# A decoder block on one core: two homes for the transposed softmax weights, a slot order with later transposes, and memory operands formed early in the space of input and residual

## The chip, the core and the metric

The kernel runs on one core of a Trainium2 chip. A core has five engines, each with its own queue, which it works off in order: TensorE (PE in the profile, its weight loads PEld), VectorE (DVE), ScalarE (ACT), GpSimd (POOL) and SyncE (SP), which here issues most of the transfers between HBM and the on-chip memory SBUF. TensorE writes its results to PSUM banks, from which VectorE and ScalarE evacuate them. The metric is the device time of one execution in microseconds; less is better.

## What is computed

One layer of a decoder block on a sequence of 512 tokens of width 1024, cut to what matters:

```python
u = rmsnorm(h, g_mix)
qa, ka, va, qb, kb, vb = split(u @ w_in, 6)
ya = dilated_attention(qa, ka, va)       # 8 heads of 64
yb = moba_attention(qb, kb, vb)          # 8 heads of 64, block 256
y = concat(rmsnorm(ya, g_out_dil), rmsnorm(yb, g_out_moba))
h = h + y @ w_out
# cross attention, 4 heads of 256, over 256 memory tokens
km, vm = split(rmsnorm(mem, g_mem) @ w_kv_mem, 2)
h = h + softmax(rmsnorm(h, g_cross) @ w_q @ km.T / 16) @ vm @ w_o
h = h + (silu(conv3(f @ w_gate)) * (f @ w_up)) @ w_down   # f = rmsnorm(h, g_ffn)
out = rmsnorm(h, g_final)
```

Everything is float32. Each product is made of three matmuls in the faster number format fp32r: an operand is split into a high part (a rounded copy, made by ScalarE) and a low part (the operand less its high part, made by VectorE or GpSimd), and high x high, high x low and low x high are summed in PSUM.

## The kernel before

The data lie transposed: features on the 128 partitions, the 512 tokens along the free axis. The input x is loaded into the eight tiles of `h`, which stay for the whole kernel as the residual; `X` holds their scaled high and low parts. Weights come in chunks of 128 x 1024 through the class `Weights`: SP loads a chunk into one of three `stage` buffers (line 74), ScalarE makes `hi` (line 88), VectorE or GpSimd makes `lo` (line 97); a chunk is loaded when the one three places earlier has been split.

Work that follows a matmul group is not written behind it but put into `Later` (lines 140 to 170): a chain of stages, each with a due step. TensorE's program calls `step()` after each small piece of work, and stages that are due are emitted then, into the queues of their engines. `need(token)` emits until a stage is out.

The attention is a software pipeline of 18 slots (line 780). In slot s three generators take turns: `s_steps(s)` makes the scores of head s in three pieces and puts the softmax into `Later` (a0 reduces on VectorE, a1 is the exponential on ScalarE, a2 the reciprocal and scaling; the last piece is scaled by GpSimd, line 695); `t_steps(s-1)` transposes the softmax weights of head s-1 in three groups (line 710, TensorE), with a copy by ScalarE (the high part) and a subtraction by VectorE (the low part, line 254) behind each; `o_steps(s-2)` multiplies the transposed weights of head s-2 with V in four pieces (line 739). The string `ORDER` says whose turn it is at each of the ten places of a slot. Ahead of each place `fill` runs some pieces of other work (an eighth of a unit, mostly three matmuls), as the table `PACE` demands: the projections `qk_unit` and `vb_unit` of later heads, and at the end, from about slot 11 on, the memory units `km_unit` (line 561) and `vm_unit` (lines 588 to 590). Accumulators of these units take turns in two PSUM banks (`acc`); scores, transposes and outputs share six others.

The memory operands are the memory, transposed and scaled, split into high and low parts. They are formed in `mem_prep` from two raw chunks, that pass through the `stage` buffers, into the tiles `X`, when the last projection (the unit k7) has read its eighth of X: one copy by ScalarE and one operation by VectorE (line 261, `X<-stage`) for each of the eight.

After the slots come the output projection with both group norms (its first addition to `h` is GpSimd's, line 832, the second VectorE's, line 840), cross attention, the feed-forward part and the final norm. These are not changed.

Of the kernel before, what the change touches and what calls it, by code (L numbers as in the profile page):

```python
# [11 lines left out]
F32 = mybir.dt.float32  # L12
# [4 lines left out]
P = 128  # L17
# [14 lines left out]
ORDER = "OSOTOSTOST"  # L32
# [140 lines left out]
def block_kernel(tc, xT, x_tok, memT, mem_tok, w_in, w_out, w_q, w_km, w_vm, w_o, w_gu, w_dn, vecs, relT, onehot,  # L173
                 addend, out):
    nc = tc.nc
    with ExitStack() as ctx:
        perm = ctx.enter_context(tc.tile_pool(name="perm", bufs=1))
        wp = ctx.enter_context(tc.tile_pool(name="wp", bufs=1))
# [24 lines left out]
        chunks += [(memT[0], "raw"), (memT[1], "raw")]  # L203
# [14 lines left out]
        hh_ = perm.tile([P, KT, S], F32, name="h")  # L218
        h = [hh_[:, k, :] for k in range(KT)]
        nc.scalar.dma_start(vec, vecs)  # L220
        nc.sync.dma_start(h[0], xT[0])
        W.dma(0)
        nc.sync.dma_start(h[1], xT[1])
        W.dma(1)
        for k in (2, 3):
            nc.sync.dma_start(h[k], xT[k])
# [17 lines left out]
        def col(c):  # L244
            return vec[:, c:c + 1]
# [121 lines left out]
        def x_split(k):  # L367
            copy(Xh[k], h[k], col(C_MIX + k))
            scaled_lo(Xl[k], h[k], col(C_MIX + k), Xh[k])
# [40 lines left out]
        for k in range(KT):  # L410
            if k % 2 == 0:
                w = W.take()
            for j in XL.get(k, ()):
                nc.sync.dma_start(h[j], xT[j])
# [29 lines left out]

        Q, K, VM = {}, {}, {}
# [12 lines left out]
        def qk_unit(p, is_k):  # L458
            hook = p == 7 and is_k
            w = W.take()  # L460
            ps = bank("acc")
            for k in range(KT):
                if hook and k == 0:
                    mem_start()
                proj(w, k, ps, Xh[k], Xl[k])
                if hook:
                    L.chain(*mem_prep(k), d=1)
                yield
# [76 lines left out]
        def mem_start():  # L545
            W.lo_eng = tuple(engs[c] for c in LOM)
            VM["st"] = [W.raw(), W.raw()]

        def mem_prep(k):

            src = VM["st"][k // 4][:, (k % 4) * M:(k % 4) * M + M]
            hi, lo = X[k][:, 0, 0:M], X[k][:, 0, M:2 * M]
            return (lambda: copy(hi, src, col(C_MEM + k)),
                    lambda: scaled_lo(lo, src, col(C_MEM + k), hi))

        def km_unit(m):
            w = W.take()
            ps = bank("acc")[:, :M]
            for k in range(KT):
                W.tick(k)  # L560
                fgroup(ps, w, k, X[k][:, 0, 0:M], X[k][:, 0, M:2 * M], k == 0, k == KT - 1)
                if k % 2 == 1:
                    L.step()
                    yield
            hi, lo = X[m][:, 1, 0:M], X[m][:, 1, M:2 * M]
            v = {}

            def e0():
                v["q"] = tmp()[:, :M]
                mul(v["q"], ps, Rm)  # L570

            L.chain(e0, lambda: copy(hi, v["q"]), lambda: sub(lo, v["q"], bf(hi)))

        def vm_unit(c):
# [71 lines left out]
        for u in (qk_unit(0, 0), qk_unit(0, 1)):  # L646
            for _ in u:
# [56 lines left out]
        def t_steps(hh):  # L704
            pt = PT[hh]
            L.need(tok["p", hh])
            for g in range(3):
# [6 lines left out]
                hi, lo = (t[:, o:o + n] for t in pts[g])  # L714
# [14 lines left out]
        def o_steps(hh):  # L729
# [50 lines left out]
        for s in range(18):  # L780
# [6 lines left out]
            if s == 16:  # L787
                ra_tok = L.chain(*norm_stages(SSQ[0], SSQ[0], S, 512), gap=3)
# [8 lines left out]
        att.close()  # L797
        cr = ExitStack()
# [472 lines left out]
```

## Time and profile before

| | |
|---|---|
| time, median of 3 runs | 796.68 us (796.01 to 797.83) |
| the profiled execution | 796.25 us, of which its span (first to last instruction) 794.5 us |
| TensorE (PE) busy | 772.7 us, 97% of the span, 3916 matmuls |
| VectorE (DVE) | 491.7 us, 62% |
| ScalarE (ACT) | 388.7 us, 49% |
| GpSimd (POOL) | 162.6 us, 20% |
| transfers | 85.86 MB, mean 108 GB/s |

Busy time is the time in which an engine has an instruction in work. Matmuls overlap, so a busy TensorE is not one at its peak: what tells whether it waited is the time from the start of one matmul to the start of the next. A row of the timeline gives start, duration, engine, line, operation, what is written and read, and in brackets how long the engine was idle before and which engine and line ended that. The table of waits sums these by waiting and releasing line.

### The profile page before, as it was taken

The page shows a single profiled execution, that of the slowest core. Times are in us where ns is not written, and L with a number is a line of the kernel's source. Part 1 is how long each engine was busy: PE and PEld are TensorE (multiplying, and loading weights), DVE is VectorE, ACT ScalarE, POOL GpSimd, SP SyncE. Part 2 cuts the span into 40 slices and gives each one's busy share as a digit, 9 for nine tenths or more (in the row PEclk, how much of TensorE's full clock was granted, in tenths as well). Part 3 has the DMA queues.
Part 4 walks back from the last instruction along what each step waited for, and adds up shares of the span by engine and source line. Part 5 has one row for each costly group of instructions (what it writes and reads, how often), then busy time and mean ns, then how long its engine had stood idle before and what let it go on. Part 6 is the DMA issues. An engine that isn't in the chain of part 4 may idle for free.

```text
span 794.5 us, 10594 instructions
## 1 busy us (share of the span) xinstructions
PE 772.7 (97%) x3916; PEld 653.9 (82%) x3916; DVE 491.7 (62%) x895; ACT 388.7 (49%) x763; POOL 162.6 (20%) x161
## 2 busy tenths in 40 slices
PE   9999999999999999999999999999999999999995
PEld 7878989877898887888888888888888888888884
DVE  4657676678886987756476765665665664333324
ACT  5856666776767543544355533334333343322322
POOL 1057465663646243000030000000000000000001
PEclk9999999999999999999999999999999999999998
DMA  9545243343534322211232323223223233333303
GB/s 344 198 133 138 78 145 93 109 112 123 161 134 131 108 80 85 75 53 54 80 106 92 104 97 106 99 87 104 91 98 106 88 92 100 99 93 100 99 21 106
DMA packets 27108, 85.86 MB, mean 108 GB/s; under 512 B 3072, under 2 KB 5248, under 8 KB 26672
## 3 DMA queue, kind: packets, MB, share of 16 engines
q1 hardware_dynamic: 25696, 83.90, 32.8%
q10 hardware_dynamic: 1232, 1.12, 0.4%
q8 instruction: 31, 0.51, 0.3%
q14 instruction: 21, 0.17, 0.1%
q0 software_dynamic: 128, 0.17, 0.1%
HBM read 78.84 MB, written 2.14 MB: 102 GB/s over the span
## 4 chain that ended last, share of the span: by engine, by line
PE 77%; DVE 11%; ACT 6%; issue 2%; POOL 2%; DMA 1%; DVEq 0%; POOLq 0%; ACTq 0%
PE acc L267 15%; PE acc L266 15%; PE acc L268 15%; PE s L267 6%; PE s L266 6%; PE s L268 6%; DVE lo L97 2%; ACT P L688 2%; PE o L739 1%; DVE tmp L257 1%; PE t L710 1%; DVE P L695 1%; DVE P L683 1%; ACT hi L88 1%; PE acc L531 1%
## 5 line engine op out<-in xcount | busy, mean ns | idle before, releaser
L88 ACT ACTIVATE hi<-stage 128x512 fp32r<-128x512 f32 (+1 forms) x264 | 151.9, 616 | 173.0 <-PE acc L267 126.6
L97 DVE TENSOR_TENSOR lo<-stage,hi 128x512 fp32r<-128x512 f32 (+1 forms) x211 | 154.8, 764 | 59.4 <-ACT hi L88 59.2
L266 PE MATMUL acc<-X,hi 128*128 128x512 f32 (+1 forms) x416 | 159.5, 384 | 1.1 <-DVE tmp L257 1.1
L268 PE MATMUL acc<-X,lo 128*128 128x512 f32 (+1 forms) x416 | 155.5, 374 | 0.0
L267 PE MATMUL acc<-X,hi 128*128 128x512 f32 (+1 forms) x368 | 137.3, 373 | 1.8 <-DVE X L261 1.5
L268 PEld LDWEIGHTS acc<-X,lo 128*128 128x128 f32 x416 | 78.2, 188 | 14.2
L266 PEld LDWEIGHTS acc<-X,hi 128*128 128x128 f32 x416 | 78.4, 188 | 13.8 <-ACT P L688 1.0
L267 PEld LDWEIGHTS acc<-X,hi 128*128 128x128 f32 x368 | 69.3, 188 | 13.1 <-DVE X L261 3.1
L97 POOL TENSOR_TENSOR lo<-stage,hi 128x512 fp32r<-128x512 f32 x53 | 71.6, 1368 | 27.3 <-ACT hi L88 25.7
L266 PE MATMUL s<-X,hi 128*128 128x512 f32 x192 | 75.1, 391 | 0.0
L268 PE MATMUL s<-X,lo 128*128 128x512 f32 x192 | 74.7, 389 | 0.0
L266 PE MATMUL acc<-G,hi 128*128 128x512 f32 (+1 forms) x198 | 72.9, 368 | 0.0
L268 PE MATMUL acc<-G,lo 128*128 128x512 f32 (+1 forms) x198 | 72.3, 365 | 0.0
L267 PE MATMUL acc<-G,hi 128*128 128x512 f32 (+1 forms) x198 | 72.3, 365 | 0.0
L267 PE MATMUL s<-X,hi 128*128 128x512 f32 x176 | 68.5, 389 | 0.0
L688 ACT ACTIVATE P<-P,st 128x512 f32<-128x512 f32 (+1 forms) x64 | 35.6, 557 | 39.9 <-DVE st L683 39.7
L1072 DVE SCALAR_TENSOR_TENSOR c<-a,vec,c 128x512 f32<-128x512 f32 x44 | 33.1, 752 | 25.2 <-ACT c L1067 24.4
L1062 POOL MEMSET a<- 128x2 f32 x22 | 2.1, 99 | 214.8 <-DVE c L1072 214.0
L266 PEld LDWEIGHTS acc<-G,hi 128*128 128x128 f32 x198 | 37.3, 188 | 6.2
L266 PEld LDWEIGHTS s<-X,hi 128*128 128x128 f32 x192 | 36.0, 187 | 7.7 <-issue 0.2
L268 PEld LDWEIGHTS acc<-G,lo 128*128 128x128 f32 x198 | 37.3, 188 | 6.1
L267 PEld LDWEIGHTS acc<-G,hi 128*128 128x128 f32 x198 | 37.3, 188 | 6.0
(249 smaller groups left out, 1498.8 us busy)
## 6 DMA issues: line engine op xcount, KB each, us to landing
stage<-in_w_gu_dram SPq DMA_DIRECT2D x44, 512.0 KB, 3.3
stage<-in_w_in_dram SPq DMA_DIRECT2D x23, 512.0 KB, 3.5
stage<-in_w_dn_dram SPq DMA_DIRECT2D x16, 512.0 KB, 3.5
strip<-scr SPq DMA_DIRECT2D x16, 256.0 KB, 3.6
stage<-in_w_km_dram SPq DMA_DIRECT2D x8, 512.0 KB, 3.3
stage<-in_w_vm_dram SPq DMA_DIRECT2D x8, 512.0 KB, 3.4
stage<-in_w_out_dram SPq DMA_DIRECT2D x8, 512.0 KB, 3.2
stage<-in_w_q_dram SPq DMA_DIRECT2D x8, 512.0 KB, 3.2
```

The lines of the kernel that those rows point to most:

```text
L88: self.nc.scalar.activation(self.hi[i][:, a:b], self.stage[i][:, a:b], AF.Copy)
L97: self.lo_eng[part].tensor_sub(self.lo[i][:, a:b], self.stage[i][:, a:b], bf(self.hi[i][:, a:b]))
L257: nc.vector.tensor_mul(dst, a, b)
L266: nc.tensor.matmul(ps, wh[:, w0:w0 + P], xh, start=first, stop=False)
L267: nc.tensor.matmul(ps, wh[:, w0:w0 + P], xl, start=False, stop=False)
L268: nc.tensor.matmul(ps, wl[:, w0:w0 + P], xh, start=False, stop=last)
L531: nc.tensor.matmul(ps, Xh[k][:, ts], wh[:, ws], start=(k == 0), stop=False)
L683: nc.vector.tensor_tensor_reduce(v, src, sb[:, :n][:, ::-1], -0.125, 3e38, OP.add, OP.min, accum_out=st[:, i:i + 1])
L688: nc.scalar.activation(v, v, AF.Exp, scale=-1.0, bias=st[:, i:i + 1], accum_out=st[:, 4 + i:5 + i])
L695: engs[NME[i]].tensor_scalar(v, v, st[:, 8 + i:9 + i], None, op0=OP.mult)
L710: nc.tensor.transpose(ps[:, c * P:(c + 1) * P], pt[:, PO[i] + kb * P:PO[i] + (kb + 1) * P], ident)
L1072: nc.vector.scalar_tensor_tensor(v["c"], v["a"][:, 6 + o:6 + o + S], col(C_CW + o * FT + f), v["c"], op0=OP.mult, op1=OP.add)
```

## The change

1. `ORDER` goes from "OSOTOSTOST" to "OOSOOTSTST". With places counted from 0, O stood at 0, 2, 4, 7, S at 1, 5, 8, T at 3, 6, 9; now O stands at 0, 1, 3, 4, S at 2, 6, 8, T at 5, 7, 9.
2. The transposed weights get a second set of tiles; even and odd heads use one each.
3. The memory operands are formed in slots 3 to 7, by the same sixteen operations, but from four loads of 256 KB of their own (tile `mr`, one buffer) and into a tile of their own, `xm`. That tile lies in the space in which the input x lay; after the last memory unit the space is taken by the residual `h`, for which x is loaded a second time (eight transfers of 256 KB on SP's queue). The two raw chunks no longer pass through the `stage` buffers. GpSimd makes both low halves of the weights until the first memory unit begins, not until the unit k7 begins.
4. The norm of the first eight heads has its stages 5 steps apart instead of 3, and the memory set aside for transfers that GpSimd issues is 2048 bytes.

```diff
-ORDER = "OSOTOSTOST"
+ORDER = "OOSOOTSTST"
...
-        chunks += [(memT[0], "raw"), (memT[1], "raw")]
...
-        hh_ = perm.tile([P, KT, S], F32, name="h")
-        h = [hh_[:, k, :] for k in range(KT)]
+        x_ = hp.tile([P, KT, S], F32, tag="H", name="x")
+        x = [x_[:, k, :] for k in range(KT)]
...
+        XM = hp.tile([P, KT, 2 * M], F32R, tag="H", name="xm")
+        def mem_prep(j):
+            v = {}
+            def p0():
+                v["t"] = tp.tile([P, 2 * M], F32, tag="mr", bufs=1, name=f"mr{j}")
+                nc.sync.dma_start(v["t"], memT[j // 2][:, (j % 2) * 2 * M:(j % 2 + 1) * 2 * M])
+            def p1(i):
+                hi, src = XM[:, 2 * j + i, 0:M], v["t"][:, i * M:(i + 1) * M]
+                copy(hi, src, col(C_MEM + 2 * j + i))
+            def p2(i):
+                hi, lo, src = XM[:, 2 * j + i, 0:M], XM[:, 2 * j + i, M:2 * M], v["t"][:, i * M:(i + 1) * M]
+                scaled_lo(lo, src, col(C_MEM + 2 * j + i), hi)
+            L.chain(p0, d=68 + 22 * j)
+            L.chain(lambda: p1(0), lambda: p2(0), lambda: p1(1), lambda: p2(1), d=80 + 22 * j, gap=2)
+        for j in range(4):
+            mem_prep(j)
...
         def qk_unit(p, is_k):
-            hook = p == 7 and is_k
...
-                if hook and k == 0:
-                    mem_start()
                 proj(w, k, ps, Xh[k], Xl[k])
-                if hook:
-                    L.chain(*mem_prep(k), d=1)
...
-                fgroup(ps, w, k, X[k][:, 0, 0:M], X[k][:, 0, M:2 * M], k == 0, k == KT - 1)
+                fgroup(ps, w, k, XM[:, k, 0:M], XM[:, k, M:2 * M], k == 0, k == KT - 1)
...
-        pts = [(ap_.tile([P, 512], F32R, name="pt0h"), ap_.tile([P, 512], F32R, name="pt0l")),
-               (ap_.tile([P, 384], F32R, name="pt1h"), ap_.tile([P, 384], F32R, name="pt1l")),
-               (ap_.tile([P, 512], F32R, name="pt2h"), ap_.tile([P, 512], F32R, name="pt2l"))]
+        pts = [[tuple(ap_.tile([P, n], F32R, name=f"pt{g}{z}{e}") for z in "hl")
+                for g, n in enumerate((512, 384, 512))] for e in range(2)]
...
-                hi, lo = (t[:, o:o + n] for t in pts[g])
+                hi, lo = (t[:, o:o + n] for t in pts[hh % 2][g])
...
-                                     pts[pg][z][:, a:b], start=(kb == 0 and z == 0),
+                                     pts[e][pg][z][:, a:b], start=(kb == 0 and z == 0),
...
-                ra_tok = L.chain(*norm_stages(SSQ[0], SSQ[0], S, 512), gap=3)
+                ra_tok = L.chain(*norm_stages(SSQ[0], SSQ[0], S, 512), gap=5)
...
+        hh_ = hp.tile([P, KT, S], F32, tag="H", name="h")
+        h = [hh_[:, k, :] for k in range(KT)]
+        for k in range(KT):
+            nc.sync.dma_start(h[k], xT[k])
...
-    nc = _bacc.Bacc("TRN2", target_bir_lowering=False, num_devices=1)
+    nc = _bacc.Bacc("TRN2", target_bir_lowering=False, num_devices=1, dynamic_dma_scratch_size=2048)
```

What stands in a row on the engines is shown at three places. Line numbers of the kernel after are 1 to 17 higher. First TensorE in slot 10, where the transposes of head 9 begin (P9 its softmax weights, t a transposes' bank, o the output of head 8, pt its transposed weights, acc a projection). Before:

```order
L739 MATMUL o_127_1742<-pt1h_428,V2_711 128x384
L739 MATMUL o_127_1742<-pt1l_429,V2_711 128x384
L266 MATMUL acc_128_1746<-X2_108,hi21_1559 128x512
L267 MATMUL acc_128_1746<-X2_108,hi21_1559 128x512
L268 MATMUL acc_128_1746<-X2_108,lo21_1590 128x512
L710 MATMUL t_131_1779<-ident_85,P9_1640 128x128 x4
L266 MATMUL acc_128_1746<-X3_109,hi21_1559 128x512
L267 MATMUL acc_128_1746<-X3_109,hi21_1559 128x512
L268 MATMUL acc_128_1746<-X3_109,lo21_1590 128x512
L739 MATMUL o_127_1742<-pt2h_430,V2_711 128x256
L739 MATMUL o_127_1742<-pt2l_431,V2_711 128x256
```

and now:

```order
L752 MATMUL o_127_1778<-pt2h0_434,V2_722 128x256
L752 MATMUL o_127_1778<-pt2l0_435,V2_722 128x256
L267 MATMUL acc_128_1782<-X3_112,hi21_1594 128x512
L268 MATMUL acc_128_1782<-X3_112,hi21_1594 128x512
L269 MATMUL acc_128_1782<-X3_112,lo21_1625 128x512
L752 MATMUL o_127_1778<-pt2h0_434,V2_722 128x256
L752 MATMUL o_127_1778<-pt2l0_435,V2_722 128x256
L267 MATMUL acc_128_1782<-X4_113,hi21_1594 128x512
L268 MATMUL acc_128_1782<-X4_113,hi21_1594 128x512
L269 MATMUL acc_128_1782<-X4_113,lo21_1625 128x512
L723 MATMUL t_132_1834<-ident_88,P9_1687 128x128 x4
```

The first transposes stood behind the second piece of O and the third eighth of the projection (X2); now all four pieces of O and the fifth eighth (X4) stand ahead of them.

Second VectorE, from the evacuation of q7 on (the unit k7 runs on TensorE, and head 12's scores begin). Before, with the memory operations `X<-stage` between the rest:

```order
L254 TENSOR_TENSOR pt2l_431<-t_146_1941,pt2h_430 128x384
L514 TENSOR_TENSOR Q7_1951<-tmp_149_1962,Q7_1951 64x512
L261 SCALAR_TENSOR_TENSOR X0_106<-stage24_1602,vec_71,X0_106 128x256
L261 SCALAR_TENSOR_TENSOR X1_107<-stage24_1602,vec_71,X1_107 128x256
L97 TENSOR_TENSOR lo27_1984<-stage27_1895,hi27_1953 128x512
L261 SCALAR_TENSOR_TENSOR X2_108<-stage24_1602,vec_71,X2_108 128x256
L683 ISA P12_1992,st12_1993<-s_151_1994,strip12_1754 128x512
L683 ISA st12_1993 128x1
L261 SCALAR_TENSOR_TENSOR X3_109<-stage24_1602,vec_71,X3_109 128x256
L693 RECIPROCAL st12_1993<-st12_1993 128x1
L695 TENSOR_SCALAR P12_1992<-P12_1992,st12_1993 128x512
L261 SCALAR_TENSOR_TENSOR X4_110<-stage25_1692,vec_71,X4_110 128x256
```

and now:

```order
L255 TENSOR_TENSOR pt2l0_435<-t_147_1976,pt2h0_434 128x384
L535 TENSOR_TENSOR Q7_1983<-tmp_149_1994,Q7_1983 64x512
L696 ISA P12_2026,st12_2027<-s_151_2028,strip12_1801 128x512
L696 ISA st12_2027 128x1
L706 RECIPROCAL st12_2027<-st12_2027 128x1
L708 TENSOR_SCALAR P12_2026<-P12_2026,st12_2027 128x512
L773 TENSOR_TENSOR y5_2048<-o_150_2008,tmp_152_2049 64x512
L258 TENSOR_TENSOR tmp_154_2063<-acc_148_1984,rx_2_141 128x512
```

The memory operations are gone from here, and the addition y, which ends an output, has come forward to the first scaling.

Third VectorE in slot 15, around the last scores (P15) and the first evacuations of the memory values (vml). Before:

```order
L760 TENSOR_TENSOR y6_2436<-o_191_2485,tmp_199_2592 64x512
L97 TENSOR_TENSOR lo37_2608<-stage37_2425,hi37_2600 128x512
L261 SCALAR_TENSOR_TENSOR Y6_123<-y6_2436,vec_71,Y6_123 128x512
L683 ISA P15_2498,st15_2499<-s_201_2619,strip15_2156 128x128
L683 ISA st15_2499 128x1
L683 ISA P15_2498,st15_2499<-s_201_2619,strip15_2156 128x256
L683 ISA st15_2499 128x1
L693 RECIPROCAL st15_2499<-st15_2499 128x2
L261 SCALAR_TENSOR_TENSOR vml_2512<-acc_197_2567,small_87,vmh_2511 128x256
```

and now:

```order
L773 TENSOR_TENSOR y6_2395<-o_191_2501,tmp_195_2568 64x512
L262 SCALAR_TENSOR_TENSOR Y6_126<-y6_2395,vec_74,Y6_126 128x512
L262 SCALAR_TENSOR_TENSOR vml_2523<-acc_192_2524,small_90,vmh_2522 128x256
L696 ISA P15_2536,st15_2537<-s_199_2596,strip15_2186 128x384
L696 ISA st15_2537 128x1
L255 TENSOR_TENSOR pt0l0_431<-t_196_2577,pt0h0_430 128x512
L706 RECIPROCAL st15_2537<-st15_2537 128x1
L708 TENSOR_SCALAR P15_2536<-P15_2536,st15_2537 128x384
L97 TENSOR_TENSOR lo35_2628<-stage35_2440,hi35_2622 128x512
L255 TENSOR_TENSOR pt1l0_433<-t_200_2609,pt1h0_432 128x384
L696 ISA P15_2536,st15_2537<-s_201_2636,strip15_2186 128x128
```

The addition y6 and the scaling Y6 stood right ahead of the third piece's reductions (128x128 and 128x256); now they stand ahead of the second piece's (128x384).

## Rows read from the trace of the kernel before

**Rows 1.** Busy time by stretch: stretch, PE, PEld, DVE, ACT, POOL, clock, DMA share, GB/s.

```profile
47.00:262.00 215.00, 206.17 (x1312) 183.58 (x1311) 155.54 (x367) 148.52 (x338) 120.39 (x103) 1.00 0.40 123
105.00:165.00 60.00, 59.87 (x356) 52.47 (x355) 41.89 (x101) 39.91 (x94) 35.08 (x32) 1.00 0.39 116
165.00:210.00 45.00, 40.77 (x245) 34.60 (x244) 35.97 (x85) 32.71 (x76) 24.73 (x22) 1.00 0.41 126
```

**Rows 2.** Waits of TensorE: waiting line, releasing line, total us, times, longest.

```profile
PE t L710 <- POOL P L695: 4.0, 7, 0.8
PE acc L588 <- DVE vml L261: 1.6, 1, 1.6
PE acc L267 <- DVE X L261: 1.5, 3, 0.8
PE acc L266 <- DVE tmp L257: 1.1, 2, 0.6
PE acc L533 <- POOL lo L97: 0.7, 1, 0.7
```

**Rows 3.** Timeline of TensorE at head 0's first transposes.

```profile
56.50 0.39 PE L267 MATMUL acc<-X,hi 128*128 128x512 f32 x1
56.73 0.39 PE L268 MATMUL acc<-X,lo 128*128 128x512 f32 x1
57.86 0.33 PE L710 MATMUL t<-ident,P 128*128 128x128 f32 x1 [0.75 <-POOL P L695]
58.77 0.33 PE L710 MATMUL t<-ident,P 128*128 128x128 f32 x1 [0.58 <-POOL P L695]
```

**Rows 4.** Timelines of TensorE and VectorE at the first memory unit; VectorE's operation (min/median/max ns).

```profile
189.53 0.28 PE L739 MATMUL o<-pt2l,V 128*128 128x256 f32 x1
189.65 0.28 PE L266 MATMUL acc<-X,hi 128*128 128x256 f32 x1
190.07 0.38 PE L267 MATMUL acc<-X,hi 128*128 128x256 f32 x1
...
196.02 0.28 PE L266 MATMUL acc<-X,hi 128*128 128x256 f32 x1
196.44 0.39 PE L267 MATMUL acc<-X,hi 128*128 128x256 f32 x1
...
188.87 2.56 DVE L261 SCALAR_TENSOR_TENSOR X<-stage,vec,X 128x256 fp32r<-128x256 f32 x2 [0.50 <-ACT X L251]
...
L261 DVE SCALAR_TENSOR_TENSOR X<-stage,vec,X x8: 472/478/1490, 188.9 to 196.3; 128x256 fp32r<-128x256 f32 x8
```

**Rows 5.** Timelines: third transposes of heads 8 and 14, their subtraction, head 8's output.

```profile
161.72 0.49 PE L710 MATMUL t<-ident,P 128*128 128x128 f32 x3
...
165.76 0.55 DVE L254 TENSOR_TENSOR pt2l<-t,pt2h 128x384 fp32r<-128x384 f32 x1
...
168.20 0.28 PE L739 MATMUL o<-pt2h,V 128*128 128x256 f32 x1
...
237.78 0.49 PE L710 MATMUL t<-ident,P 128*128 128x128 f32 x3
...
243.25 0.55 DVE L254 TENSOR_TENSOR pt2l<-t,pt2h 128x384 fp32r<-128x384 f32 x1
```

**Rows 6.** Timeline of slot 15: Y, the last scores' reduction, the value unit's wait.

```profile
239.03 1.48 DVE L261 SCALAR_TENSOR_TENSOR Y<-y,vec,Y 128x512 fp32r<-128x512 f32 x1 [0.22 <-ACT Y L251]
...
240.54 0.29 DVE L683 CUSTOM_DVE_ANT_0 P<-s,strip 128x128 f32<-128x128 f32 x1
...
242.79 0.38 PE L588 MATMUL acc<-hi,X 128*128 128x256 f32 x1 [1.57 <-DVE vml L261]
```

**Rows 7.** SP's weight load, first additions to h; loads of h: size, median to landing.

```profile
263.63 0.33 SPq L74 DMA_DIRECT2D stage<-in_w_out_dram  x1
...
267.66 1.66 POOL L832 TENSOR_TENSOR h<-h,tmp 128x512 f32<-128x512 f32 x1 [2.94 <-DVE tmp L257]
...
273.50 1.28 DVE L840 TENSOR_TENSOR h<-h,tmp 128x512 f32<-128x512 f32 x1
...
h<-in_xT_dram SPq DMA_DIRECT2D x8, 256.0 KB, 6.3
```

More of the change, by code (lines that the diff above doesn't have):

```diff
@@ L177, in block_kernel @@
         perm = ctx.enter_context(tc.tile_pool(name="perm", bufs=1))
+        hp = ctx.enter_context(tc.tile_pool(name="hp", bufs=1))
         wp = ctx.enter_context(tc.tile_pool(name="wp", bufs=1))
@@ L217, in block_kernel @@
         vec = perm.tile([P, NVEC], F32, name="vec")
-        hh_ = perm.tile([P, KT, S], F32, name="h")
-        h = [hh_[:, k, :] for k in range(KT)]
+        x_ = hp.tile([P, KT, S], F32, tag="H", name="x")
+        x = [x_[:, k, :] for k in range(KT)]
         nc.scalar.dma_start(vec, vecs)
-        nc.sync.dma_start(h[0], xT[0])
+        nc.sync.dma_start(x[0], xT[0])
         W.dma(0)
-        nc.sync.dma_start(h[1], xT[1])
+        nc.sync.dma_start(x[1], xT[1])
         W.dma(1)
         for k in (2, 3):
-            nc.sync.dma_start(h[k], xT[k])
+            nc.sync.dma_start(x[k], xT[k])
         W.dma(2)
@@ L367, in x_split @@
         def x_split(k):
-            copy(Xh[k], h[k], col(C_MIX + k))
-            scaled_lo(Xl[k], h[k], col(C_MIX + k), Xh[k])
+            copy(Xh[k], x[k], col(C_MIX + k))
+            scaled_lo(Xl[k], x[k], col(C_MIX + k), Xh[k])
         def tok_load(src, n):
@@ L413, in block_kernel @@
             for j in XL.get(k, ()):
-                nc.sync.dma_start(h[j], xT[j])
+                nc.sync.dma_start(x[j], xT[j])
             if k in XT:
@@ L542, in vb_unit @@
                 tok["v", g, t] = L.chain(*v_evac(V[g][t], ps, rcol[:, t:t + 1]))
[L545 to L554, printed above, removed]
         def km_unit(m):
+            if m == 0:
+                W.lo_eng = tuple(engs[c] for c in LOM)
             w = W.take()
@@ L585, in vm_unit @@
                     ws = slice((k % 4) * 256, (k % 4) * 256 + 256)
-                    xh = X[k][:, 0, t * P:(t + 1) * P]
-                    xl = X[k][:, 0, M + t * P:M + (t + 1) * P]
+                    xh = XM[:, k, t * P:(t + 1) * P]
+                    xl = XM[:, k, M + t * P:M + (t + 1) * P]
                     nc.tensor.matmul(ps, xh, wh[:, ws], start=(k == 0), stop=False)
@@ L648, in block_kernel @@
                 pass
-        pts = [(ap_.tile([P, 512], F32R, name="pt0h"), ap_.tile([P, 512], F32R, name="pt0l")),
-               (ap_.tile([P, 384], F32R, name="pt1h"), ap_.tile([P, 384], F32R, name="pt1l")),
-               (ap_.tile([P, 512], F32R, name="pt2h"), ap_.tile([P, 512], F32R, name="pt2l"))]
-        for t in pts[2]:
-            nc.vector.memset(bf(t[:, 0:128]), 0.0)
+        pts = [[tuple(ap_.tile([P, n], F32R, name=f"pt{g}{z}{e}") for z in "hl")
+                for g, n in enumerate((512, 384, 512))] for e in range(2)]
+        for e in range(2):
+            for t in pts[e][2]:
+                nc.vector.memset(bf(t[:, 0:128]), 0.0)
         PT, stat = {}, {}
```

## The prediction, made before the change was run

> **What bounds the kernel now.** I read the engines by stretch first [rows 1]. TensorE's columns are the ones to look at: in the attention stretch, 47 to 262 us, it is busy 206.17 of 215 us, so 8.8 us are idle; from 105 to 165 us next to nothing (0.13 us), from 165 to 210 us 4.23 us. The granted clock is 1.00 in all three rows, the higher level. After that I read who TensorE waited for [rows 2]: in this stretch nearly all of it is for the transposes T (line 710, 4.0 us in seven waits, for POOL's part of the softmax normalisation), for a memory value unit (line 588, 1.6 us), and for single accumulators and weights. The matmul count is not changed, so only such waits can be won or made. VectorE is the engine to watch beside it: 35.97 of 45 us busy (80%) from 165 to 210 us, against 70% from 105 to 165 us.
>
> One correction to these rows. Matmuls without a wait start 0.23 us apart though each is drawn 0.39 us long (56.50 and 56.73 us in [rows 3]), so a pause is drawn about 0.16 us shorter than it is: from 56.73 to 57.86 us there are 1.13 us between starts, 0.90 more than 0.23, and the row says 0.75. I count by starts.
>
> **The later transposes (ORDER).** T of head s-1 moves from places 3, 6, 9 of a slot to 5, 7, 9; O of head s-2 from 0, 2, 4, 7 to 0, 1, 3, 4. The last piece of S keeps place 8. Counted in the two orders (0.23 us for a matmul of 512 columns, 0.12 for 256), the work between the last S and the first T grows by 1.3 us in head 0 and by 1.8 to 2.7 us in the others. The two halves of the worst waits come to 0.75 + 0.58 us [rows 3], plus 0.32 by starts, about 1.7 us, of which the 1.3 us of head 0 cover most and the 1.8 of the others all. All seven waits: 4.0 + 7 x 0.16 = 5.1 us, taken in full; 4.0 is the lower bound.
>
> The price is on the other side. The way from T to the O that uses it shrinks: the second group's from 5.5 to 7.9 us of matmuls to 3.5 to 5.0 us, the third's from 4.6 to 7.3 us to 3.6 to 6.3 us. What must fit in is ScalarE's copy and VectorE's subtraction, queued behind other work. In head 8 the third transposes start at 161.72 us and VectorE's part ends at 165.76 + 0.55 = 166.31 us, 4.6 us later; O came at 168.20 us [rows 5], in time only because TensorE waited for the next T meanwhile. The new order has 3.6 us of matmuls there: a wait of 1.0 us. In head 14, 237.78 to 243.25 + 0.55, it is 6.0 us against 3.9 [rows 5], but there the 1.6 us of line 588 are in it. Setting every head's lag as it is now against its new way, seven of the 32 second and third groups come short, by 7.0 us together; 5.0 of that is in heads 11 and 14, whose lags contain the memory work and the wait of line 588, both won below, and 2.0 is left. Bounds 0 and 7.0; I take 2.5.
>
> The second home of the transposed weights takes a write-after-read wait away that has no cause in the new order: O has read its last piece (place 4) before the next T (place 5). 0 us; its two more fills of zeros happen once, beside the first projections on TensorE.
>
> **The memory operands.** Now ScalarE and VectorE form them while the unit that needs them runs: VectorE has to fit eight operations between its other work from 188.87 us on [rows 4]. The first matmul of each eighth does not need the low part, the second does. Without a wait, starts are 0.12 us apart (189.53 to 189.65); to the second matmul it is 0.42 us (189.65 to 190.07, and the same from 196.02 to 196.44), and the four pairs between stretch likewise [rows 4]. The six pairs sum to 3.60 us, less 6 x 0.12 = 2.9 us won. Lower bound 1.5 us, what the waits for X alone are drawn as. Next in line there is the accumulator wait of 0.6 us on line 266 behind the same backlog [rows 2]; 0.7 us by starts.
>
> The same eight operations on each engine now stand in slots 3 to 7 (about 95 to 150 us). VectorE's take 0.48 us alone and up to 1.49 us [rows 4]. Their cover is VectorE's 30% of idle time from 105 to 165 us [rows 1]: 8 x 0.48 = 3.8 us in 18 us. If the cover fails it is 3.8 us; I take 0.3. The four loads of 256 KB go through SP's queue; each waits for the last reader of the load before it, and strips, K copies and weights queue behind it. Two loads of 512 KB that held two of the three stage buffers until this unit are gone, which speaks for earlier weights, not later ones.
>
> **The vml wait.** Line 588 waits at 242.79 us because the last S's reduction on VectorE came only at 240.54 us, behind the 1.48 us of Y (line 261, at 239.03) [rows 6]; ScalarE's exponentials and the evacuation follow it in order. In the new order y and Y stand ahead of the second S piece, half a slot earlier, since O ends at place 4. 1.6 + 0.16 = 1.7 us won; bounds 0 and 1.7.
>
> **h read again.** x, the memory operands and h now share one space, so h is loaded eight times 256 KB after the last value matmul, behind the weight load that in the trace is issued at 263.63 us [rows 7]. Even with the 6.3 us to landing of the crowded start, h[0] is there at 263.63 + 0.33 + 6.3 = 270.3 us; POOL's first addition (now at 267.66 us, 1.66 us long) would end at 271.9 us, before VectorE's at 273.50 us needs it. The next ones are needed every 24 x 0.23 = 5.5 us. Cost 0; without that cover 2.6 us (270.3 less 267.66). The smaller scratch of POOL's transfers has no row that prices it; its four early transfers end long before attention, and I take 0.
>
> **The sum.** Won 5.1 + 2.9 + 0.7 + 1.7 = 10.4 us. Paid 2.5 (O) + 0.3 (memory work in slots 3 to 7) + 1.0 for new meetings of the kind of the 0.7 us of line 533 [rows 2], which any new order brings. Net 6.6 us. The profiled run took 796.25 us: 789.65 us; the median of the runs is 0.43 us above it: **790.1 us**.
>
> **Rivals.**
> (1) *The shortened way to O takes most of it.* All seven short places cost their 7.0 us and the other two payments shrink to 0.4: net 3 us, 793.7 us. For it: head 8's lag. Against it: the longest lags are made by what goes.
> (2) *Slower: the second half of a slot becomes VectorE's.* S, T, S, T stand within places 6 to 9, and with them two reductions, two scalings and three subtractions in one queue. The second groups' mean new way is 4.5 us. If each lags 5.4 us, 16 x 0.9 = 14.4 us are paid: 14.4 + 1.3 - 10.4 = 5.3 us lost, 802.0 us. It decides from a lag of 5.1 us in every head on. For it: third groups now lag up to 6.0 us [rows 5]. Against it: fourteen of the sixteen second groups lag 1.9 to 4.3 us now.
> (3) *The waits only move.* VectorE is 80% busy from 165 to 210 us; a TensorE that arrives earlier at one place waits at the next for the same queue. Only the memory's 2.9 us are won, and 2 us of it are paid: 795.8 us. For it: every wait of rows 2 is for VectorE or what stands behind it. Against it: over the whole stretch VectorE has a quarter of its time free.
> (4) *Memory work collides with POOL.* The first two memory operations took 2.56 us together, against 0.48 each in later ones [rows 4], while POOL was at work. At 1.49 us each, eight cost 8.1 us more of VectorE between 95 and 150 us; with their own 3.8 us its share would go from 70% to 90%, beyond the 80% at which TensorE idled 4.23 us in 45. I price it at 4 us: 794.1 us. The Trainium skill (SBUF — State Buffer, section Who interferes with whom) says that a VectorE instruction with two SBUF inputs contends with a GpSimd instruction that reads SBUF; by that rule these operations, whose source and high part both lie in SBUF, can meet POOL wherever they are put, and the trace agrees with its 1.49 against 0.48 us.
>
> **Chances.** Forecast 0.56; (1) 0.15; (4) 0.05; (3) 0.13; (2) 0.11. A run can tell 0.2%, 1.6 us, from no change; the forecast, (1) and (4) are faster by more, (3) lies within, (2) is slower. The range: low 796.7 - 10.4 = 786.3 us (all won, nothing paid), high 795.9 us, which takes in (1), (4) and (3) and leaves out (2).
>
> **What would show it.** T: no wait for POOL's line of the normalisation. O: the wait, if any, stands at the second and third groups for VectorE's subtraction. Memory: no wait for its low parts, which lie between 95 and 150 us. Line of the value unit: no wait behind Y. TensorE's idle time from 47 to 262 us goes from 8.8 us to about 3. The forecast is wrong if O's waits sum to over 5 us, or if 105 to 165 us, now without idle time, shows some.

## The result and the profile after

The changed kernel takes 791.96 us (median of 5 runs, 791.42 to 793.15) against 796.26 us; the ratio is 0.9943, with a 95% interval of 0.9932 to 0.9954. That is 4.3 us faster, inside the predicted range and 1.9 us above the predicted time. The profiled execution took 792.2 us, of which 790.2 us are its span.

Busy time by stretch (columns as in [rows 1]), first for the whole attention stretch and then for two parts of it:

```profile
47.00:262.00 215.00, 209.52 (x1333) 187.59 (x1332) 159.64 (x369) 150.90 (x343) 125.06 (x105) 1.00 0.41 128
105.00:165.00 60.00, 57.87 (x344) 50.09 (x343) 42.68 (x106) 41.56 (x97) 36.29 (x31) 1.00 0.37 115
165.00:210.00 45.00, 43.23 (x280) 39.12 (x279) 37.79 (x81) 32.19 (x73) 27.34 (x23) 1.00 0.41 121
```

TensorE's idle time in the first row went from 8.83 to 5.48 us, where the prediction expected about 3. From 165 to 210 us it fell from 4.23 to 1.77 us, but from 105 to 165 us it rose from 0.13 to 2.13 us, where there had been none. Waits of TensorE (waiting line, releasing line, total us, times, longest):

```profile
PE o L752 <- DVE pt0l L255: 1.8, 1, 1.8
PE t L303 <- DVE tmp L255: 1.2, 1, 1.2
PE acc L552 <- DVE V L262: 1.1, 1, 1.1
...
PE o L752 <- DVE pt1l L255: 0.9, 3, 0.5
PE acc L600 <- DVE vml L262: 0.6, 1, 0.6
```

The first line of [rows 2], the transposes' 4.0 us for POOL, is gone, and so is the wait for the memory's low parts; the value unit's wait for vml is down from 1.6 to 0.6 us. New are O's waits (line 752), one for an evacuation of V (line 552), and a longer one for the second residual norm (line 303; it was 0.6 us).

Two timelines show where the new waits come from. The first is VectorE before the longest wait of O, with POOL's two instructions at the same time and then TensorE's matmul:

```profile
204.74 0.75 DVE L262 SCALAR_TENSOR_TENSOR Y<-y,vec,Y 128x512 fp32r<-128x512 f32 x1 [0.34 <-ACT Y L252]
205.41 1.78 DVE L97 TENSOR_TENSOR lo<-stage,hi 128x512 fp32r<-128x512 f32 x1
207.12 1.50 DVE L255 TENSOR_TENSOR X<-tmp,X 128x256 fp32r<-128x256 f32 x1
208.54 0.55 DVE L696 CUSTOM_DVE_ANT_0 P<-s,strip 128x384 f32<-128x384 f32 x1
...
209.02 0.68 DVE L255 TENSOR_TENSOR pt0l<-t,pt0h 128x512 fp32r<-128x512 f32 x1
...
205.30 1.34 POOL L282 TENSOR_TENSOR ssy<-ssy,tmp 128x512 f32<-128x512 f32 x1 [2.96 <-ACT tmp L277]
206.61 1.73 POOL L97 TENSOR_TENSOR lo<-stage,hi 128x512 fp32r<-128x512 f32 x1
...
209.75 0.50 PE L752 MATMUL o<-pt0l,V 128*128 128x512 f32 x1 [1.77 <-DVE pt0l L255]
```

VectorE does Y, a weight's low part and a km operand, the latter two stretched while POOL is at work (1.78 and 1.50 us, where the same forms take 0.68 and 0.42 us at other places), and only then the reduction and the subtraction that O needs. The second is VectorE before the wait for V, then ScalarE's copy of V, then TensorE:

```profile
120.92 1.51 DVE L262 SCALAR_TENSOR_TENSOR xm<-mr,vec,xm 128x256 fp32r<-128x256 f32 x1
...
122.96 0.47 DVE L262 SCALAR_TENSOR_TENSOR xm<-mr,vec,xm 128x256 fp32r<-128x256 f32 x1
...
127.41 0.42 DVE L696 CUSTOM_DVE_ANT_0 P<-s,strip 128x256 f32<-128x256 f32 x1
...
128.34 0.49 ACT L701 ACTIVATE P<-P,st 128x256 f32<-128x256 f32 x1
...
128.83 0.46 ACT L252 ACTIVATE V<-acc,small 128x256 fp32r<-128x256 f32 x1
...
129.95 0.35 PE L552 MATMUL acc<-hi,X 128*128 128x256 f32 x1 [1.15 <-DVE V L262]
```

Two memory operations (xm), 1.98 us together, stand ahead of the reductions of S; ScalarE's exponentials wait for those, and V's copy stands behind the exponentials in ScalarE's queue. The loads of the raw memory (tile mr) were late as well:

```profile
L262 DVE SCALAR_TENSOR_TENSOR xm<-mr,vec,xm x8: 466/552/1511, 82.4 to 123.0; 128x256 fp32r<-128x256 f32 x8
...
  DMA mr<-in_memT_dram: 4.7, 2
...
DMA to landing us min/median/max: 3.5/3.6/6.8
```

The first line gives VectorE's eight operations (min/median/max ns, first and last start), the second what the operations on this tile waited for: ScalarE stood idle 4.7 us, in two waits, until a load had landed. The third is the time from issue to landing.

A table of sums is used below. By starts, the excess of a stretch is the time from each matmul's start to the next beyond the usual one of its form (0.23 us for 512 columns, 0.12 for 256), summed over all matmuls in it; each row is the profiled execution of one kernel, in us. The kernels e5, e7, e9 and e12 are those of the experiments, where each is named.

| stretch, us | before | new order, 5 steps (e5) | after | e7 | e9 | e12 |
|---|---|---|---|---|---|---|
| 50 to 80 | 3.3 | 1.1 | 1.1 | 1.1 | 1.1 | 1.1 |
| 80 to 110 | 0.3 | 0.4 | 1.1 | 0.4 | 0.4 | 0.4 |
| 110 to 140 | 0.6 | 0.2 | 2.7 | 2.4 | 0.9 | 0.9 |
| 140 to 180 | 2.4 | 1.3 | 1.3 | 1.2 | 1.3 | 1.2 |
| 180 to 220 | 6.5 | 7.2 | 2.2 | 2.1 | 2.2 | 0.6 |
| 220 to 250 | 2.3 | 2.0 | 2.0 | 2.0 | 2.0 | 1.7 |
| 250 to 270 | 0.9 | 1.6 | 1.5 | 1.5 | 1.6 | 1.4 |
| whole span | 23.2 | 20.6 | 18.9 | 17.1 | 16.3 | 13.7 |

### The profile page after: what moved, and what is told of

Same layout as the page of the kernel before. It is cut to its first block, busy times and chain, and to the rows that moved or that the text cites. A ratio compares the mean times of both kernels' runs of the same rounds, so it can differ in the third digit from the quotient of the medians.

```text
span 790.2 us, 10599 instructions
## 1 busy us (share of the span) xinstructions
PE 771.4 (98%) x3916; PEld 653.9 (83%) x3916; DVE 491.9 (62%) x896; ACT 388.4 (49%) x763; POOL 164.7 (21%) x162
## 3 DMA queue, kind: packets, MB, share of 16 engines
HBM read 80.93 MB, written 2.14 MB: 105 GB/s over the span
## 4 chain that ended last, share of the span: by engine, by line
PE 80%; DVE 9%; ACT 5%; issue 2%; DMA 2%; POOL 1%; DVEq 0%; SPq 0%; ACTq 0%; POOLq 0%
PE acc L267 17%; PE acc L268 16%; PE acc L269 16%; PE s L268 6%; PE s L269 6%; PE s L267 6%; DVE lo L97 2%; PE o L752 2%; DVE tmp L258 1%; DMA mr<-in_memT_dram 1%; PE t L723 1%; POOL h L849 1%; ACT P L701 1%; ACT hi L88 1%; PE s L690 1%
## 5 line engine op out<-in xcount | busy, mean ns | idle before, releaser
L97 DVE TENSOR_TENSOR lo<-stage,hi 128x512 fp32r<-128x512 f32 x210 | 154.0, 764 | 60.7 <-ACT hi L88 60.5
L267 PE MATMUL acc<-X,hi 128*128 128x512 f32 x352 | 140.4, 399 | 0.5 <-DVE tmp L258 0.5
L269 PE MATMUL acc<-X,lo 128*128 128x512 f32 x352 | 137.5, 391 | 0.0
L268 PE MATMUL acc<-X,hi 128*128 128x512 f32 x304 | 118.6, 390 | 0.0
L269 PEld LDWEIGHTS acc<-X,lo 128*128 128x128 f32 x352 | 66.1, 188 | 14.2
L97 POOL TENSOR_TENSOR lo<-stage,hi 128x512 fp32r<-128x512 f32 x54 | 73.9, 1385 | 17.5 <-ACT hi L88 15.0
L267 PEld LDWEIGHTS acc<-X,hi 128*128 128x128 f32 x352 | 66.2, 188 | 12.3 <-DVE tmp L258 1.0
L268 PEld LDWEIGHTS acc<-X,hi 128*128 128x128 f32 x304 | 57.1, 188 | 9.8 <-issue 0.2
```

The source lines that it names most:

```text
L97: self.lo_eng[part].tensor_sub(self.lo[i][:, a:b], self.stage[i][:, a:b], bf(self.hi[i][:, a:b]))
L267: nc.tensor.matmul(ps, wh[:, w0:w0 + P], xh, start=first, stop=False)
L268: nc.tensor.matmul(ps, wh[:, w0:w0 + P], xl, start=False, stop=False)
L269: nc.tensor.matmul(ps, wl[:, w0:w0 + P], xh, start=False, stop=last)
```

## The experiments

Each kernel was timed in five rounds beside the kernel before, whose median was 796.2 to 796.4 us each time.

**The order alone, and the change without the order.** The first (e1) is the kernel before with one line changed, the second (e2) the changed kernel with that line changed back:

```diff
-ORDER = "OSOTOSTOST"
+ORDER = "OOSOOTSTST"
```

> The kernel before with the new ORDER alone: one home for the transposed weights, the memory operands formed late as before. Theory A (the two parts add up, and the 1.9 us that TensorE now loses at 123 to 130 us to late evacuations of V are the price of the memory work there): the T waits go (5.3 us), 0.4 us of the value unit's wait goes, O waits come (3.3 us) and the residual norm's matmul waits 0.6 us longer; net 1.8 us won, about 794.5 us against 796.3, and no wait for V at 123 to 130 us. Rival B (those V waits are made by the order, since S now stands later in the slot): the 1.9 us stand here too, about 796.4 us, no change. Rival C (the old late memory work at 188 us collides with the new order): its waits of 2.9 us grow, 797 us or more.

> The changed kernel with the old ORDER: two homes, memory operands formed in slots 3 to 7, h read again. Theory A: 3.6 us won where the memory operands were formed (2.9 and 0.7), 1.9 us paid for V's evacuations at 123 to 130 us, T waits of 4 us as before; about 794.6 us against 796.3. Rival B (the V waits belong to the order): no such waits, 792.7 us. Rival D (the two homes or the early memory work also shorten the T waits): below 792 us.

Measured: the order alone 798.32 us (ratio 1.0018, 1.0010 to 1.0027), the change without the order 799.54 us (1.0038, 1.0025 to 1.0051). Both halves are slower than before, and together they are faster; no expectation that lets the parts add up fits. In the first, the waits of TensorE begin with one that neither before nor after has:

```profile
PE acc L266 <- DVE vml L261: 3.9, 1, 3.9
PE o L739 <- DVE pt0l L254: 2.1, 1, 2.1
```

It is the first matmul of the output projection, whose accumulator a memory value unit still holds. No V wait stood at 123 to 130 us there, so rival B fell; and the 0.6 us that theory A adds at the norm's matmul did not come. In the second run that norm's wait had grown:

```profile
PE t L723 <- POOL P L708: 5.7, 8, 1.7
PE t L303 <- DVE tmp L255: 2.6, 1, 2.6
```

Both hints point to the end of the attention stretch, where the change has a fourth part that the prediction had given no price: the stages of the first eight heads' norm 5 steps apart instead of 3.

**One home, and 3 steps again.** In the changed kernel:

```diff
-                for g, n in enumerate((512, 384, 512))] for e in range(2)]
+                for g, n in enumerate((512, 384, 512))] for e in range(1)] * 2
-        for e in range(2):
+        for e in range(1):
```

```diff
-                ra_tok = L.chain(*norm_stages(SSQ[0], SSQ[0], S, 512), gap=5)
+                ra_tok = L.chain(*norm_stages(SSQ[0], SSQ[0], S, 512), gap=3)
```

> The changed kernel with one home for the transposed weights. Theory: the second home is worth nothing in this order, since O has read its last piece one place before the next T; 792.0 us, within 0.2% of the changed kernel, and no wait of ScalarE's or VectorE's copies on O. Rival: TensorE's last O matmul and the copy of the next T meet, ScalarE's copy waits for it at some heads and the O waits grow by up to 0.2 us a head, 795 us.

> The changed kernel with the stages of the residual norm 3 steps apart, as before, instead of 5. Theory: TensorE's wait for that norm's reciprocal row (1.2 us at line 303, excess by starts 1.4 us at 262 us) goes back to the 0.8 us of before or less; 0.6 us won, 791.4 us. Rival: the stages only come earlier into the same busy VectorE queue and delay the last y and O: no change or up to 1 us lost.

One home (e3): 791.93 us, the same as after. Three steps (e4): 795.93 us (0.9990, 0.9981 to 0.9999), 4.0 us more than after, where 0.6 us less was expected and 1 us more was the rival. The 3.9 us wait is there too. Timelines of ScalarE, VectorE and TensorE in that run:

```profile
251.87 1.28 ACT L307 ACT_TABLE_LOAD   x1
253.16 0.69 ACT L307 ACTIVATE tmp<-t,small 128x512 f32<-128x512 f32 x1
...
254.43 0.71 ACT L252 ACTIVATE Y<-y,vec 128x512 fp32r<-128x512 f32 x1
...
255.17 0.75 DVE L262 SCALAR_TENSOR_TENSOR Y<-y,vec,Y 128x512 fp32r<-128x512 f32 x1 [2.49 <-ACT Y L252]
255.93 0.69 DVE L312 SCALAR_TENSOR_TENSOR tmp<-t,tmp 128x512 f32<-128x512 f32 x1
...
257.37 1.65 DVE L258 TENSOR_TENSOR ssy<-tmp,tmp 128x512 f32<-128x512 f32 x1
258.94 0.47 DVE L262 SCALAR_TENSOR_TENSOR vml<-acc,small,vmh 128x256 fp32r<-128x256 f32 x1
...
259.46 0.80 PE L267 MATMUL acc<-Y,hi 128*128 128x512 f32 x1 [3.92 <-DVE vml L262]
260.06 0.63 PE L268 MATMUL acc<-Y,hi 128*128 128x512 f32 x1
```

The norm's table load and two activations (251.87 to 254.5 us) stand ahead of the last Y in ScalarE's queue, and its three VectorE operations ahead of the vml that frees the accumulator. With 5 steps, in the trace after, the same six instructions stand behind that Y and that vml (table load at 256.27 us, VectorE's three from 259.71 us on), and TensorE does not wait there. And the wait costs more than its length: the next matmuls start 0.43 us apart instead of 0.23, as the clock (the column before the last two) shows:

```profile
255.00:260.00 5.00, 1.08 (x6) 0.84 (x5) 4.75 (x7) 3.98 (x9) 2.59 (x2) 0.84 0.00 2
260.00:264.00 4.00, 4.00 (x11) 3.08 (x10) 1.60 (x4) 0.00 (x0) 0.00 (x0) 0.50 0.75 253
```

**The two missing corners.** The kernel before with the new order and 5 steps (e5); the changed kernel with the old order and 3 steps (e6).

> The kernel before with the new ORDER and the stages of the residual norm 5 steps apart; memory operands late, one home. Theory: the 3.9 us wait for vml's low part at 255 us, which the new ORDER alone made and after which the granted clock fell to the lower level for some us, comes from the norm's ScalarE work (a table load and two activations) standing ahead of the last Y and of the value unit's evacuations; with 5 steps it stands behind them. So this run is 4.3 us faster than the new ORDER alone: 794.0 us. Rival (the wait is that of the late memory work, pushed to the end of the attention stretch): no change from 798.3 us.

> The changed kernel with the old ORDER and the residual norm's stages 3 steps apart: two homes and early memory operands alone. Theory: with the old ORDER the 5 steps cost 2.1 us (TensorE's wait at line 303 for the second norm's row, 2.6 us against 0.6), so this run is 797.4 us: slower than before, because the early memory work costs TensorE 4.7 us between 110 and 140 us and wins less than that at 188 to 196 us. Rival (the gap does nothing in the old ORDER): 799.5 us.

Measured: 793.68 us (0.9963, 0.9949 to 0.9976), as the theory said, and 796.30 us (0.9996, 0.9988 to 1.0005), no change from before and 1.1 us below what was expected. Medians of all corners in us; the lower row is the changed kernel, so that it holds the second home, the second load of h, the smaller scratch memory and GpSimd's longer share of the low parts too:

| | old order, 3 steps | old order, 5 steps | new order, 3 steps | new order, 5 steps |
|---|---|---|---|---|
| memory operands late | 796.3 (before) | not run | 798.3 | 793.7 |
| memory operands early | 796.3 | 799.5 | 795.9 | 792.0 (after) |

The steps are worth 4.6 and 4.0 us won in the new order and cost 3.2 us in the old one. Of that the trace shows 2.0 us as the wait of line 303 (2.6 against 0.6 us). The rest goes with the granted clock: three of e2's six executions, at a mean granted clock of 0.994 to 0.995, take 798.3 to 798.9 us, 2.1 us more in the median than e6's at 0.994 to 0.996, and the other three, at 0.990 to 0.991, take 800.2 to 800.5 us. What lowered it in those three is not shown, as the kept trace is of one of the first three.

The lower row wins 1.7 us beside the new order with 5 steps, and nothing beside the old one with 3. There the excess by starts, as in the table of sums, tells why: from before to e6 it falls from 6.5 to 1.3 us at 180 to 220 us, but it rises from 0.6 to 5.4 us at 110 to 140 us. A transpose waits 1.7 us for GpSimd's scaling at 120 us there, a wait that no run of the new order has, and the granted clock is lower after it (what delays that scaling was not followed):

```profile
120.00:124.00 4.00, 3.18 (x11) 2.60 (x12) 2.33 (x6) 3.15 (x7) 3.19 (x4) 0.64 0.05 16
```

**Earlier loads; later memory work.** Both with one home, since it costs nothing, and two buffers for the raw loads:

```diff
-                v["t"] = tp.tile([P, 2 * M], F32, tag="mr", bufs=1, name=f"mr{j}")
+                v["t"] = tp.tile([P, 2 * M], F32, tag="mr", bufs=2, name=f"mr{j}")
...
-            L.chain(p0, d=68 + 22 * j)
+            L.chain(p0, d=48 + 22 * j)
```

The second run has d=145 + 16 * j for the loads and d=165 + 16 * j for the operations (80 + 22 * j before).

> The changed kernel with one home, and the four loads of the memory's raw operand issued 20 steps earlier into two buffers; the operations that read them stay where they are. Theory A (ScalarE's two waits for these loads, 4.7 us together, and what queues behind them make TensorE's waits of 0.6 us at 91 us and of 1.9 us at 123 to 130 us): 790.0 to 791.3 us. Theory B (the waits at 123 to 130 us come from VectorE's queue, where a memory operation of 1.5 us beside POOL stands ahead of the S reduction): only the 0.3 to 0.6 us at 91 us go, 791.5 us, and the waits at 123 to 130 us stay.

> The changed kernel with one home, loads 20 steps ahead in two buffers, and the memory operands formed in slots 7 to 10 (about 132 to 165 us), clear of the evacuation of the last V unit. Theory B (memory work collides with V's evacuations at 123 to 130 us): those 1.9 us go and little takes their place, since TensorE has no idle time from 130 to 160 us now: about 790 us. Rival (VectorE's queue is the limit wherever the work stands): the waits come again at other places as O waits at the third groups, 792 us.

Earlier loads (e7): 790.93 us (0.9925, 0.9911 to 0.9938), 1.0 us less than after. ScalarE waits for no load any more, and the excess at 80 to 110 us went from 1.1 to 0.4 us (table); in e3 and e4, whose loads stand as in after, it is 0.8 and 0.6 us, so what late loads cost differs between executions. The waits at 122 to 128 us stayed: theory A had the time, B the place. Later work (e8): 795.48 us (0.9988, 0.9978 to 0.9999), 4.6 us worse than the run beside it, against both expectations. Its stretches and waits:

```profile
160.00:164.00 4.00, 1.33 (x7) 0.64 (x5) 3.18 (x6) 1.91 (x4) 1.32 (x1) 1.00 0.42 131
164.00:168.00 4.00, 3.56 (x9) 2.64 (x10) 3.33 (x12) 3.46 (x11) 1.30 (x2) 0.61 0.19 55
...
PE o L752 <- DVE pt0l L255: 3.6, 2, 1.9
...
PE o L752 <- ACT pt0h L250: 1.2, 1, 1.2
```

The V waits were gone, as theory B has it, but two memory operations of 1.5 us each now stood ahead of the first group's subtraction, and the clock fell after the waits that they made. VectorE there:

```profile
158.01 1.50 DVE L262 SCALAR_TENSOR_TENSOR xm<-mr,vec,xm 128x256 fp32r<-128x256 f32 x1
...
161.69 1.49 DVE L262 SCALAR_TENSOR_TENSOR xm<-mr,vec,xm 128x256 fp32r<-128x256 f32 x1
...
163.70 0.69 DVE L255 TENSOR_TENSOR pt0l<-t,pt0h 128x512 fp32r<-128x512 f32 x1
```

TensorE had no idle time at 130 to 160 us before; that was no sign of room in VectorE's queue.

**Denser memory work, an earlier second norm, low parts on POOL.** All three on top of the earlier loads:

```diff
-            L.chain(p0, d=48 + 22 * j)
+            L.chain(p0, d=60 + 16 * j)
...
-            L.chain(lambda: p1(0), lambda: p2(0), lambda: p1(1), lambda: p2(1), d=80 + 22 * j, gap=2)
+            L.chain(lambda: p1(0), lambda: p2(0), lambda: p1(1), lambda: p2(1), d=80 + 16 * j, gap=2)
```

```diff
-        rb_tok = L.chain(*norm_stages(RB, RB, S, 512), d=RBD, gap=2)
+        rb = norm_stages(RB, RB, S, 512)
+        L.chain(*rb[:2], d=RBD - 2, gap=1)
+        rb_tok = L.chain(*rb[2:], d=RBD + 4, gap=2)
```

```diff
-LOM = "vg"
+LOM = "gg"
```

> One home, raw memory loads 20 steps ahead in two buffers, and the memory operations 16 steps apart instead of 22, so that the last of them ends about 10 us before the last V unit (from 122 us). Theory: the waits for V's evacuations at 122 to 128 us (2.2 us by starts) were made by the last memory group ahead of the S reduction in VectorE's queue and go; the earlier groups still meet no short path: 788.7 us, against 790.9 us with 22 steps. Rival: the groups now meet the K and Q evacuations and the T of slots 3 to 5 and cost as much there: 791 us.

> One home, loads early, memory operations 22 steps apart, and the first two stages of the second residual norm (a copy on ScalarE, a subtraction on VectorE) two and three steps earlier; its matmuls stay where they are. Theory: TensorE's wait at 260 us (1.4 us by starts, for that subtraction, which stood behind two weight low parts and a product) falls to 0 to 0.3 us: 789.6 us against 790.9. Rival: the copy waits for its input, or the product behind the subtraction is late for its reader: 790.9 us or more.

> One home, loads early, and both halves of the weights' low parts on POOL in the memory units too, instead of one on VectorE. Theory A (O's wait at 206 us of 1.9 us and the value unit's waits of 1.3 us at 230 to 236 us come from VectorE's queue being too full): they go, 788 us. Theory B (POOL's extra 1.35 us each slow VectorE's operations beside it, 0.48 to 1.5 us, and the weights come later): TensorE waits for POOL's low parts, 793 us or more.

Denser (e9): 789.33 us (0.9916, 0.9902 to 0.9929). The memory operations end by 113 us, none of them is long any more, and the excess at 110 to 140 us falls from 2.4 to 0.9 us:

```profile
L262 DVE SCALAR_TENSOR_TENSOR xm<-mr,vec,xm x8: 471/479/673, 81.2 to 112.4; 128x256 fp32r<-128x256 f32 x8
```

Earlier norm (e10): 790.94 us, no change. Its wait is gone from TensorE's list, but the wait of the output projection for VectorE's products doubled, to 1.1 us in two:

```profile
PE acc L267 <- DVE tmp L258: 1.1, 2, 0.8
```

The excess by starts at 260 us fell by 1.2 us and rose by 1.1 us from 290 to 310 us: the wait had only moved. Low parts on POOL (e11): 788.74 us (0.9906, 0.9891 to 0.9921). The waits for pt0l (1.7 us in the run with earlier loads) and vml (0.6 us) are gone from TensorE's list, one of 0.7 us for POOL's low part has come:

```profile
PE acc L602 <- POOL lo L97: 0.7, 1, 0.7
```

**Two of the gains together.**

> Both of the last gains together: memory operations 16 steps apart with early loads and one home, and the low parts of the memory units' weights on POOL alone. Theory (the two take away different waits, at 122 to 128 us and at 206 us, so they add): 788.7 less 1.7 us, 787.1 us. Rival (TensorE arrives earlier at 206 to 236 us and waits for POOL's low parts instead): 788.7 us, no change from the better of the two.

Measured (e12): 786.95 us (0.9882, 0.9865 to 0.9898), 9.4 us below the kernel before and 5.0 us below the changed one; the two gains add up. Its attention stretch:

```profile
47.00:262.00 215.00, 211.79 (x1347) 190.23 (x1346) 152.17 (x360) 153.18 (x346) 142.62 (x122) 1.00 0.43 136
```

## Why the prediction was right, and where it was not

The sign and the range held, and the main gains came as described. By its own test one thing failed: it called itself wrong if 105 to 165 us showed idle time, and 2.13 us of it are there. O's waits, its other test, stayed under the 5 us (3.8 us by starts).

**The transposes.** 5.1 us were forecast and 5.7 us won, counted by starts over all seven waits and the shorter pauses beside them: no wait for line 708 is left. In the table it is most of the fall at 50 to 80 us; at 140 to 180 us it is 1.8 us, of which a new wait of O takes 0.7 back, and the rest lies in the row from 180 us on.

**The memory operands.** 2.9 + 0.7 us were forecast; by starts, with the pauses of 0.1 us behind them, 4.3 us stood there. From e5 to after, which differ by the early memory work (and by the second home, which is worth nothing, and one weight's low part more on GpSimd near 187 us, which no run parts off), 180 to 220 us fell from 7.2 to 2.2 us: 5.0 us, because in e5 a wait of O at 197 us (1.4 us by starts) goes as well.

**The work in slots 3 to 7: the term that was mis-sized.** Forecast 0.3 us, at most 3.8; measured 3.0 us (80 to 140 us: 0.9 before, 3.8 after), of which 1.7 us are the two waits of line 552 (for the accumulator at 124 us and for V at 130 us) and 1.2 us short waits of O. It lay at 82 to 123 us, not at 95 to 150. The step that failed is "Their cover is VectorE's 30% of idle time". The idle time was there: over the 55 us that hold this work and what it delayed, VectorE's share rose from 70 to 74%, and in e9 it is 74% too, with 0.4 us paid instead of 3.0. In this order, before, after and e9:

```profile
80.00:135.00 55.00, 54.91 (x347) 49.28 (x347) 38.76 (x92) 35.71 (x84) 31.10 (x28) 1.00 0.35 107
```

```profile
80.00:135.00 55.00, 53.04 (x325) 46.21 (x324) 40.87 (x95) 37.68 (x88) 29.60 (x26) 1.00 0.37 115
```

```profile
80.00:135.00 55.00, 54.67 (x346) 48.79 (x344) 40.82 (x100) 39.58 (x92) 30.26 (x28) 1.00 0.40 126
```

What counted was which work stood behind each operation. Runs e7 and e9 part the sum: 1.0 us goes with earlier loads (3.8 to 2.8), 1.5 us with the last pair moved away from the reductions of S from 125 us on (2.8 to 1.3), and 0.4 us is left. Rival (4) named a part of it: one of the eight operations is stretched from 0.47 to 1.51 us (in the trace POOL is at its weights' low parts from 119.42 to 122.15 us). The Trainium skill (SBUF — State Buffer, section Who interferes with whom) says that a VectorE instruction with two SBUF inputs contends with a GpSimd instruction that reads SBUF; the trace agrees, with 466 and 1511 ns for one form. The other seven take 0.47 to 0.67 us, not the 1.49 us each that it reckoned with for its 4 us. What the stretch cost and what the place cost is not parted, since e9 changed both.

**O.** Forecast 2.5 us; measured 3.0 us outside of 80 to 140 us, with the pauses of 0.1 us behind the waits. In e9 the two waits of O that are left come to 2.5 us (0.6 at 161 and 1.9 at 205 us). The sum was right and its place was not: the longest wait is for a first group, which the prediction had not counted among the short ones, and e11 shows why it is there: with VectorE's half of the weights' low parts on POOL it is gone. That the sum came near is in part luck. The prediction kept every head's lag as it was; from the start of a group's transposes to the end of its subtraction, the mean over the 16 heads went from 3.5 to 4.5 us in the second groups and from 3.7 to 4.6 us in the first.

**The vml wait: won and given back.** 1.7 us were forecast as won. The wait at 242.79 us [rows 6], 1.8 us by starts, did go; but the value units now wait at 232, 235 and 237 us, the longest again for vml, 1.7 us together with the pauses behind them. ScalarE's copy of vm stands there behind the exponentials of the last S piece (236.72 + 0.50 us, then 237.22 us in ScalarE's timeline), as it did before. The prediction moved Y out of the way and did not look for the next in line.

**The norm's steps: the term that was missing.** The prediction costed three parts of the change and of the fourth only the smaller scratch memory (0 us). The 5 steps cost 0.6 us at line 303, but without them the new order makes a wait of 3.9 us and a slow clock behind it; e4 is 4.0 us slower than after. So the forecast's sum tacitly rested on a part that it did not price. The order alone came out slower than before, for this reason and not for rival (2)'s: the loss stood at one place, not in the second half of every slot.

**Second home, h read again.** 0 us each was forecast. The home: 0.0 us (e3). For h and for the smaller scratch memory no run parts them off; POOL's first addition starts at 263.47 us, 0.09 us after the product that it also needs (262.70 + 0.68), and h's first load, issued at 258.37 us, had landed 3.5 us later, so the load was not what came last.

The account by starts, after against before: won 5.7 (T) + 4.3 (memory) + 0.1 (vml, net) + 0.3 (weights near 73 us) = 10.4 us; paid 3.0 (slots 3 to 7) + 3.0 (O) + 0.6 (norm) = 6.6 us; net 3.8 of the 4.3 us measured, the rest in pauses under 0.1 us. The forecast had 10.4 won and 3.8 paid: the price was 2.8 us too low. That the gains agree in sum is luck: T, memory and weights gave 1.6 us more than forecast, and the vml wait 1.6 us less.

## What to carry to other kernels

A small edit that rides along with a large one (here one number, 3 to 5) wants a price of its own: ask what the large edit would do without it. Before moving work into an engine's idle share, look in its queue for the instruction that stands right behind the new place and for who waits for that; an idle TensorE share of zero in a stretch says nothing about it. And when a wait on one engine comes from another engine's queue, it is worth trying the third engine: here the low parts on POOL won 2.2 us.

## What the runs showed of the hardware

After the 3.9 us wait in e4, thirteen matmuls of 512 columns took 5.72 us (259.46 to 265.18 us), 2.7 us more than at 0.23 us each; the granted clock was 0.50 from 260 to 264 us, the lower of its two levels (1.2 GHz), and the matmuls from 265.45 us on are 0.23 us apart again. A shorter wait did it in one execution and not in two others: e6, e2 and the kernel before all wait 1.6 us near 242 us for vml, and these rows are, in this order, e6 and e2:

```profile
240.00:244.00 4.00, 2.13 (x16) 1.58 (x15) 2.88 (x10) 2.25 (x8) 3.49 (x4) 1.00 0.37 131
244.00:248.00 4.00, 4.00 (x23) 4.00 (x22) 1.39 (x2) 1.75 (x3) 2.01 (x2) 0.57 0.43 131
```

```profile
240.00:244.00 4.00, 2.14 (x16) 1.59 (x14) 3.06 (x10) 2.45 (x8) 3.49 (x4) 1.00 0.42 131
244.00:248.00 4.00, 4.00 (x34) 4.00 (x35) 1.37 (x2) 2.87 (x6) 2.48 (x2) 1.00 0.34 130
```

TensorE was busy for 2.13 and 2.14 us of the first four; over the next four the granted clock was 0.57 in the mean in one and 1.00 in the other, as it was in the kernel before. What decides between them was not tried.

A load of 256 KB of raw memory took 3.5 to 6.8 us to land in the changed kernel, with a median of 3.6 us. The slow one was the first, issued right behind two copies between tiles of Y (73.45 and 74.61 us):

```profile
75.12 0.60 SPq L454 DMA_DIRECT2D mr<-in_memT_dram  x1
```

With the loads 20 steps earlier (e7) the first took 3.6 us; the second now stood right behind the same two copies and took 5.8 us, and nothing waited for it. So it was slow by its place and not as the first load; which of the transfers around it make it so was not tried.
